# mLSTM's convolution on GpSimd by way of DRAM, its gate scans in HGRN2's sixth chunk, and forget-gate attention's keys placed beside the projections

## The chip, the core and the metric

One NeuronCore of a Trainium2 chip runs the whole program. It has TensorE (matrix products; PE in the rows), VectorE (DVE), ScalarE (ACT), GpSimd (POOL) and SyncE (SP), which here only issues DMA transfers. Each engine runs its own instructions in order and waits on semaphores for the others. TensorE's clock has two levels, 1.2 and 2.4 GHz; the rows give the granted clock of a stretch as a share of the upper one. The metric is the time of one execution in microseconds (us).

## What is computed

The reference is one block with a mixer and a feed-forward part, on 1024 tokens of width 1024. The change touches the mixer alone. A projection of the normalised input gives the inputs of four mixers, each 256 wide (S5, HGRN2, forget-gate attention, mLSTM):

```
def causal_depthwise_conv(x, w):
    k_w, ch = w.shape
    return lax.conv_general_dilated(
        x, w[:, None, :].astype(x.dtype), window_strides=(1,), padding=[(k_w - 1, 0)],
        dimension_numbers=('NWC', 'WIO', 'NWC'), feature_group_count=ch)
...
def mlstm_mixer(q, k, v, o, ig, fz, conv_w, gain):
    bsz, seq, _ = q.shape
    qk = jax.nn.silu(causal_depthwise_conv(jnp.concatenate([q, k], axis=-1), conv_w))
    q_c, k_c = qk[..., :GROUP_W], qk[..., GROUP_W:]
...
    lf = jax.nn.log_sigmoid(fz.astype(F32))
...
    _, h = lax.scan(_mlstm_chunk, init,
                    (heads(q_c), heads(k_c * ML_DH ** -0.5), heads(v), gates(ig), gates(lf)))
```

The convolution has four taps over time, channel by channel, on the 512 channels of mLSTM's queries and keys, and SiLU behind it. The mLSTM gates need running sums and running maxima over the 1024 tokens. HGRN2 is a gated linear recurrence in chunks with 4 heads of 64, forget-gate attention is softmax attention with 4 heads whose scores get the difference of a cumulative log gate, `s = q k / 8 + F[t] - F[s]`.

## The kernel before

Fp32 matrices are split into a high and a low part, and a product is three matmuls (`mm3`, L100 to L102). The input x comes in eight tiles of 128 tokens (`xt`); they are normalised, transposed on TensorE and kept split in SBUF (`aT`), and then all column blocks of the input projection are made from them, in halves of 512 tokens (`gemm_half`: 24 matmuls of 128x512). A generator `g` (`gemms`) yields after each half, so that the caller lays these halves between the steps of the mixers. The order in each engine's queue is that of the program, partly rearranged by a scheduler that respects priorities. A projected block is copied out of PSUM by ScalarE, is transposed if its mixer wants the other layout (`keep_tm`, L403, copies the transposed block), and goes to DRAM scratch (`d_mqk` for mLSTM's queries and keys, `d_fk` and `d_fq` for the attention's, `d_gate` for the gates).

The stage of HGRN2 is the loop over eight chunks of 128 tokens: `hg_scores` (key transposes L832, 56 score products L840), a half of the projection, `hg_out` of the chunk before, another half, `hg_products` (L858 to L868). The level decays (`hlev`) are differences of the scanned log gate (`hb`, L776) made by GpSimd (L790, L791; 28 subtractions for a quarter of 256 tokens), an exponential by ScalarE, and products by VectorE (L797, L799). Quarters are prepared two chunks ahead.

Into this loop mLSTM's preparation is laid: `ml_gates` (rows of 1024 tokens on 4 partitions, VectorE scans L948 and L950) in chunk 0, `ml_conv` for one of the four feature tiles of 128x1024 in each of the chunks 1 to 4, and `ml_columns` (gate rows to columns, L985 and L992) in chunk 5. `ml_conv` loads the tile (`mraw`), scales it by the last tap (L928) and adds the three other taps (L930) on VectorE, takes tanh on ScalarE (L931), makes the SiLU product on VectorE (L932) and scales it on GpSimd (L934). The result stays in SBUF in `mqk0` and `mqk1`. After the loop mLSTM's chunks 0 to 2 run between the last halves of the projection (`ml_scores`: L1018 transposes a tile of keys), then the projections' memory is released and forget-gate attention's pool takes it (`fox_prep`: raw keys `f_kr`, their split `fkA`, the gate row on all partitions `fFB`, values `fv`; L1086 to L1089). `fox_tile` loads eight times four heads' queries (`f_qr`, L1102), splits them (`f_Q`, L1104 and L1105) and makes scores (`at_s`, L1110).

At the start, the constants are loaded on SyncE's queue, then two blocks of weights and x; the tiles of x lie where the constants' raw rows lay. The reciprocal root is made by VectorE in eleven small steps (L61 to L67, `rsq_a`, `rsq_y`), the scaling of x is L117, the transposition L129.

## Time and profile before

| | |
|---|---|
| median of 3 runs | 2910.1 us (2907.98 to 2913.05) |
| the profiled execution | 2912.16 us, span 2910.40 us |
| TensorE (PE) busy | 2664.5 us, 92% of the span |
| weight load (PEld) busy | 2249.0 us, 77% |
| VectorE (DVE) busy | 1836.6 us, 63% |
| ScalarE (ACT) busy | 1221.5 us, 42% |
| GpSimd (POOL) busy | 714.1 us, 25% |

The span is the time from the first to the last instruction that the profiler recorded; the shares are means over stages of different kinds, so that a stage has to be looked at by itself. A busy TensorE need not be at the full clock.

### The profile page before, as it was taken

Reading aid. Unit: us, or ns where it says so; the run is one execution under the profiler, and the core shown is the slowest. Engines: PE = TensorE matmul, PEld = TensorE weight load, DVE = VectorE, ACT = ScalarE, POOL = GpSimd, SP = SyncE. Lnnn points to the kernel's source line nnn. Section 1 sums busy time; section 2 is a strip of 40 time slices with the busy share of each in tenths; the row PEclk is TensorE's granted clock in tenths of the full one; section 3 lists DMA queues with packets and bytes.
Section 4 is the critical chain, followed back from the end, with each engine's and each line's share of the span. In section 5 each row is a group of like instructions: output and inputs, shape, how many; then the busy total and the mean of one; then the engine's idle time right before and its main releaser. Section 6 shows DMA issues by size and latency. Waiting matters only on the chain. (4 is left out here: it accounts for less than half of the span.)

```text
span 2910.4 us, 44979 instructions
## 1 busy us (share of the span) xinstructions
PE 2664.5 (92%) x16607; PEld 2249.0 (77%) x16607; DVE 1836.6 (63%) x4443; ACT 1221.5 (42%) x2362; POOL 714.1 (25%) x839
## 2 busy tenths in 40 slices
PE   6999679899999999899999999999999999699884
PEld 5677558787899878899878787888887888587773
DVE  7523885666888866989563362665653265876665
ACT  4315432344444564444643251444333122465553
POOL 6221520000577511787001000000000100322211
PEclk9899789789999999999999999999999999899997
DMA  4334332423332334323444543511113464799995
GB/s 134 76 95 120 87 92 65 131 70 132 124 112 92 109 124 130 117 88 105 138 120 119 132 122 89 130 57 48 51 35 119 175 209 151 232 305 299 314 301 194
DMA packets 336050, 388.65 MB, mean 134 GB/s; under 512 B 46962, under 2 KB 276220, under 8 KB 335684
## 3 DMA queue, kind: packets, MB, share of 16 engines
q1 hardware_dynamic: 322404, 355.65, 39.5%
q0 software_dynamic: 13280, 29.58, 3.6%
q8 instruction: 132, 2.16, 0.3%
q14 instruction: 90, 0.74, 0.1%
q10 hardware_dynamic: 144, 0.52, 0.0%
HBM read 326.83 MB, written 79.77 MB: 140 GB/s over the span
## 5 line engine op out<-in xcount | busy, mean ns | idle before, releaser
L78 DVE TENSOR_TENSOR f_w<-f_wr,f_w 128x512 fp32r<-128x512 f32 x264 | 292.6, 1135 | 55.3 <-ACT f_w L76 53.9
L100 PE MATMUL g_ps<-a_hi,wh 128*128 128x512 f32 (+1 forms) x648 | 265.8, 410 | 4.9 <-ACT wh L76 4.3
L102 PE MATMUL g_ps<-a_hi,wl 128*128 128x512 f32 (+1 forms) x648 | 260.5, 402 | 1.8 <-DVE wl L78 1.8
L101 PE MATMUL g_ps<-a_lo,wh 128*128 128x512 f32 (+1 forms) x648 | 260.1, 401 | 0.0
L76 ACT ACTIVATE f_w<-f_wr 128x512 fp32r<-128x512 f32 x264 | 158.7, 624 | 175.7 <-POOL f_wr L1324 55.6
L100 PE MATMUL f_ps<-t,f_w 128*128 128x256 f32 x704 | 203.4, 289 | 15.6 <-DVE c L1308 11.9
L102 PE MATMUL f_ps<-t,f_w 128*128 128x256 f32 x704 | 202.5, 288 | 6.5 <-DVE f_w L78 6.5
L101 PE MATMUL f_ps<-t,f_w 128*128 128x256 f32 x704 | 200.8, 285 | 0.0
L1558 ACT ACTIVATE at_sb<-at_sb,at_m 128x256 f32<-128x256 f32 (+7 forms) x224 | 142.2, 635 | 132.5 <-DVE at_m L1556 58.4
L1789 POOL TENSOR_TENSOR o<-o,on 128x256 f32<-128x256 f32 x32 | 24.5, 765 | 623.0 <-DVE at_z L1578 294.6
L78 DVE TENSOR_TENSOR wl<-wr,wh 128x1024 fp32r<-128x1024 f32 (+1 forms) x61 | 74.0, 1215 | 128.7 <-ACT wh L76 128.5
L100 PE MATMUL e_gps<-e_wh,e_xTh 128*128 128x256 f32 x528 | 153.7, 291 | 0.0
L100 PE MATMUL f_ps<-b,f_w 128*128 128x256 f32 x528 | 150.1, 284 | 3.1 <-ACT f_w L76 1.5
L101 PE MATMUL e_gps<-e_wl,e_xTh 128*128 128x256 f32 x528 | 150.8, 286 | 1.4 <-DVE e_wl L78 1.4
L100 PEld LDWEIGHTS f_ps<-t,f_w 128*128 128x128 f32 x704 | 136.6, 194 | 20.0 <-issue 15.8
L102 PE MATMUL f_ps<-b,f_w 128*128 128x256 f32 x528 | 149.4, 283 | 2.7 <-DVE f_w L78 2.7
L102 PE MATMUL e_gps<-e_wh,e_xTl 128*128 128x256 f32 x528 | 150.5, 285 | 0.0
L101 PE MATMUL f_ps<-b,f_w 128*128 128x256 f32 x528 | 149.3, 283 | 0.0
L100 PEld LDWEIGHTS g_ps<-a_hi,wh 128*128 128x128 f32 (+1 forms) x648 | 124.1, 191 | 31.8 <-ACT wh L76 5.0
L102 PEld LDWEIGHTS g_ps<-a_hi,wl 128*128 128x128 f32 (+1 forms) x648 | 123.7, 191 | 28.3 <-DVE wl L78 2.6
L102 PEld LDWEIGHTS f_ps<-t,f_w 128*128 128x128 f32 x704 | 136.6, 194 | 9.9 <-DVE f_w L78 9.8
L101 PEld LDWEIGHTS g_ps<-a_lo,wh 128*128 128x128 f32 (+1 forms) x648 | 124.1, 191 | 23.7
(688 smaller groups left out, 7763.2 us busy)
## 6 DMA issues: line engine op xcount, KB each, us to landing
e_wg<-in_w_gate_e_dram SPq DMA_DIRECT2D x33, 1024.0 KB
e_wu<-in_w_up_e_dram SPq DMA_DIRECT2D x33, 1024.0 KB
e_wd<-in_w_down_e_dram SPq DMA_DIRECT2D x33, 1024.0 KB
wr<-in_w_in_dram SPq DMA_DIRECT2D x60, 512.0 KB
f_dr<-in_w_ffn_down_dram SPq DMA_DIRECT2D x52, 512.0 KB
f_wr<-in_w_ffn_gate_dram SPq DMA_DIRECT2D x44, 512.0 KB
f_wr<-in_w_ffn_up_dram SPq DMA_DIRECT2D x44, 512.0 KB
Q<-qd SPq DMA_DIRECT2D x64, 256.0 KB
```

The lines of the kernel that those rows point to most:

```text
L76: a = self.nc.scalar.activation(hi, raw, AF.Copy)
L78: return a, (eng or self.nc.vector).tensor_tensor(lo, raw, hi.bitcast(F32), ALU.subtract)
L100: nc.tensor.matmul(ps, lh, rh, start=(j == 0), stop=False)
L101: nc.tensor.matmul(ps, lh, rl, start=False, stop=False)
L102: self.last_mm = nc.tensor.matmul(ps, ll, rh, start=False, stop=(j == n - 1))
L1558: nc.scalar.activation(p, p, AF.Exp, bias=m[:, hd:hd + 1], accum_out=z[:, hd:hd + 1])
L1789: nc.gpsimd.tensor_tensor(o4, o4, on, A)
```

## The change

The convolution is made by GpSimd alone but for the tanh, a tile in each of the chunks 0 to 3: a scaling for each tap into a second tile, an addition for the three shifted ones, one operation that makes 0.5 or 0.0625 times (tanh + 1), and one product. The result goes to new DRAM scratch `d_mqc`; `ml_rows` loads it back into `mqk0` and `mqk1` after the loop, in a pool that takes over HGRN2's memory. `ml_gates` is called in chunk 5 and not in chunk 0, `ml_columns` after the loop. `fox_prep` is called before the projections' memory is released, in a pool of its own (`foxk`) on the other side, with two buffers for the raw keys. Two smaller edits: the first four x tiles are loaded on ScalarE's queue, into memory that no longer overlaps the constants' (the two pools change places), and `keep_tm`'s 24 copies out of PSUM are made by ScalarE.

```diff
-                            tmp, early = pool("n_tmp", stack=t_), pool("n_w", 2, stack=t_)
+                            early, tmp = pool("n_w", 2, stack=t_), pool("n_tmp", stack=t_)
...
-                                nc.sync.dma_start(xt, x[t * P:(t + 1) * P, :])
+                                (nc.scalar if t < 4 else nc.sync).dma_start(xt, x[t * P:(t + 1) * P, :])
...
+                            with self.seq():
+                                self.hg_scores(d, c)
+                            decays()
+                            if c < 4:
+                                self.ml_conv(mlt, c)
+                            elif c == 5:
+                                self.ml_gates(mlt)
...
-                        if c == 0:
-                            self.ml_gates(ml, mlt)
-                        elif c < 5:
-                            self.ml_conv(ml, mlt, c - 1)
...
-                        if c == 5:
-                            with self.seq():
-                                self.ml_columns(ml)
+                            self.hg_out(d, NT - 1)
+                    hg_.close()
+                    mp = pool("ml")
+                    self.ml_rows(mp)
                     with self.seq():
-                        self.hg_out(d, NT - 1)
-                mp = pool("ml2")
+                        self.ml_columns(mp)
+                fk = pool("foxk")
...
+                self.fox_prep(fk)
 
             self.pe_last = None
             self.att = pool("fox", 3, side="right")
-            self.fox_prep()
...
-            nc.vector.tensor_copy(o, ps)
+            nc.scalar.copy(o, ps)
...
+        for j in range(4):
+            nc.sync.dma_start(self.mqk[j // 2][:, j % 2], self.d_mqc[j])
...
-        V = nc.vector
-        V.tensor_scalar(dst, src, w(3), None, op0=M)
+        G.tensor_scalar(dst, src, w(3), None, op0=M)
         for d in range(1, 4):
-            V.scalar_tensor_tensor(dst[:, d:], src[:, :T - d], w(3 - d), dst[:, d:], op0=M, op1=A)
+            G.tensor_scalar(t, src, w(3 - d), None, op0=M)
+            G.tensor_tensor(dst[:, d:], dst[:, d:], t[:, :T - d], A)
         nc.scalar.activation(src, dst, AF.Tanh, scale=0.5)
-        V.scalar_tensor_tensor(dst, src, 1.0, dst, op0=A, op1=M)
-
-        G.tensor_scalar(dst, dst, 0.5 * (0.125 if j >= 2 else 1.0), None, op0=M)
...
+        G.tensor_scalar(src, src, 1.0, 0.5 * (0.125 if j >= 2 else 1.0), op0=A, op1=M)
+        G.tensor_tensor(dst, dst, src, M)
+        nc.sync.dma_start(self.d_mqc[j], dst)
```

In the changed file the lines of mLSTM stand six lower (L931 is L936) and HGRN2's one lower (L812 is L813). The first place is ScalarE's queue at the start of HGRN2's chunk 2, where the tanh of a convolved tile (`mraw`) stands. Before, tanh of the first tile:

```order
L902 ACTIVATE hn_sq<-ho 128x256
L762 ACT_TABLE_LOAD
L762 ACTIVATE ht_3390<-ht_3390 128x512
L360 COPY g_raw<-g_ps 128x512
L931 ACT_TABLE_LOAD
L931 ACTIVATE mraw<-mqk_2343 128x1024
L875 COPY hoS<-o_ps 128x256
L768 ACTIVATE hz<-hz 128x512
```

After, tanh of the second tile, behind the exponential of the quarter's levels (`hlev`):

```order
L876 COPY hoS<-o_ps 128x256
L794 ACTIVATE hlev<-hlev 128x1792
L805 ACTIVATE hqe<-hb 128x256
L936 ACTIVATE mraw<-mcv 128x1024
L809 ACTIVATE hebl<-hb 128x2
L813 ACTIVATE hke<-hke 128x256
L361 COPY g_raw<-g_ps 128x512
L404 COPY gs<-g_tp 128x512
L834 COPY hkT<-kT_ps 128x256
```

The tanh's input is now made by GpSimd (`mcv`), and the key decay (`hke`), the copies of projected blocks (`g_raw`, `gs`) and the transposed keys (`hkT`) stand behind it.

The second place is TensorE's queue at the end of the loop, from HGRN2's last output transpose (`oT_ps`) on. Before:

```order
L868 MATMUL o_ps<-hP,hvc 64x64 x2
L888 MATMUL oT_ps<-ident,hoS 128x128 x2
L1018 MATMUL mk_ps<-ident,mqk_2343 128x128 x2
L1023 MATMUL me_ps<-mMx,msel 128x128
L1024 LDWEIGHTS identb
```

After:

```order
L889 MATMUL oT_ps<-ident,hoS 128x128 x2
L990 MATMUL mc_ps<-ident,mrows 128x128 x8
L998 MATMUL md_ps<-mdec,msel_4245 128x8
L998 MATMUL md_ps<-mdec,msel_4248 128x8
L1024 MATMUL mk_ps<-ident,mqk_4222 128x128
L1029 MATMUL me_ps<-mMx,msel 128x128
```

The columns (`mc_ps`, `md_ps`) now stand between HGRN2's last output and mLSTM's first use of `mqk`, and no half of the projection does; `mqk` is a new tile that the four loads fill.

The third place is VectorE's queue in the changed kernel at HGRN2's chunks 0 and 1, where the mLSTM gate rows (`mrows`, `mmx`, `mR`; the scans are the rows L954 and L956) stand between the masked scores of chunk 0 (`hP`), its state update (`hS`) and the next quarter's gates (`ht`, `hz`):

```order
L844 TENSOR_TENSOR hP<-sc_ps,hmask 128x448
L914 SCALAR_TENSOR_TENSOR mrows<-mrows 4x1024
L953 MEMSET mrows 4x1024
L954 SCALAR_TENSOR_TENSOR mrows<-mrows 4x1024
L765 TENSOR_SCALAR ht_2389<-hz 128x512
L955 TENSOR_TENSOR mrows<-mrows 4x1024
L874 SCALAR_TENSOR_TENSOR hS_1049<-hS_1049,hebl,o_ps 64x64 x2
L874 SCALAR_TENSOR_TENSOR hS_1050<-hS_1050,hebl,o_ps 64x64 x2
L956 SCALAR_TENSOR_TENSOR mmx<-mrows 4x1024
L959 COPY mR<-mmx 4x8
L966 TENSOR_TENSOR mrows<-mrows,mmx 4x1024
```

They stood in the same two chunks before; what the call in chunk 5 did not move is mLSTM's part of these rows.

## Rows read from the trace of the kernel before

**Rows 1.** Busy us of each engine by stretch, clock, DMA share, GB/s

```profile
320.00:330.00 10.00, 1.29 (x12) 0.90 (x12) 9.81 (x34) 4.62 (x8) 3.09 (x2) 0.69 0.50 141
...
370.00:380.00 10.00, 0.41 (x6) 0.43 (x8) 9.81 (x32) 5.57 (x9) 3.23 (x2) 0.58 0.39 114
```

**Rows 2.** TensorE's waits from 40 to 620 us: total, times, longest

```profile
PE sc_ps L840 <- DVE hlev L799: 12.3, 2, 11.7
PE md_ps L992 <- DVE mcols L985: 9.7, 1, 9.7
PE sc_ps L840 <- DVE rsq_a L66: 9.2, 1, 9.2
...
PE at_s L1110 <- ACT f_Q L1104: 3.3, 1, 3.3
```

**Rows 3.** Lines of the convolution on VectorE: min/median/max ns, first and last start

```profile
L928 DVE TENSOR_SCALAR mqk<-mraw,vcol x4: 739/740/916, 315.9 to 383.0; 128x1024 f32<-128x1024 f32 x4
...
L930 DVE SCALAR_TENSOR_TENSOR mqk<-mraw,vcol,mqk x12: 1265/1272/1277, 316.9 to 389.7; 128x1023 f32<-128x1023 f32 x4, 128x1022 f32<-128x1022 f32 x4, 128x1021 f32<-128x1021 f32 x4
...
L932 DVE SCALAR_TENSOR_TENSOR mqk<-mraw,mqk x4: 1216/1222/1227, 324.4 to 395.3; 128x1024 f32<-128x1024 f32 x4
```

**Rows 4.** The copy of the transposed block, the same columns

```profile
L403 DVE COPY gs<-g_tp x24: 658/682/692, 99.9 to 516.2; 128x512 f32<-128x512 f32 x24
```

**Rows 5.** GpSimd's operations of 128x1024: by line, and by group (busy us, mean ns)

```profile
L934 POOL TENSOR_SCALAR mqk<-mqk x4: 2760/2766/2791, 325.8 to 396.6; 128x1024 f32<-128x1024 f32 x4
...
L78 POOL TENSOR_TENSOR e_wl<-e_wg,e_wh 128x1024 fp32r<-128x1024 f32 x2 | 4.7, 2354 | 0.0
L600 POOL COPY s5u<-s5u 128x1024 f32<-128x1024 f32 x2 | 2.3, 1188 | 13.7 <-DMA s5u<-tm_u 13.7
```

**Rows 6.** GpSimd's level subtractions, group of 258 to 470 us

```profile
L790 POOL TENSOR_TENSOR hlev<-hb 128x128 f32<-128x128 f32 x42 | 24.2, 576 | 5.9 <-DVE hb L776 5.8
```

**Rows 7.** Timeline of TensorE at chunks 2 and 4: start us, us, instruction

```profile
317.65 0.27 PE L832 MATMUL kT_ps<-ident,hke 128*128 128x128 f32 x1
...
339.12 0.51 PE L858 MATMUL o_ps<-heads,hpd 128*128 128x2 f32 x4
...
366.62 0.27 PE L832 MATMUL kT_ps<-ident,hke 128*128 128x128 f32 x1
```

**Rows 8.** Timeline of VectorE beside GpSimd's scaling from 325.8 us

```profile
326.10 0.72 DVE L66 SCALAR_TENSOR_TENSOR rsq_a<-rsq_a,ms 128x4 f32<-128x4 f32 x1
...
327.89 0.15 DVE L66 SCALAR_TENSOR_TENSOR rsq_a<-rsq_a,ms 128x4 f32<-128x4 f32 x1
```

**Rows 9.** Line of HGRN2's scans: min/median/max ns

```profile
L776 DVE TENSOR_TENSOR_SCAN hb<-ones,ht x16: 391/433/5510, 105.7 to 402.3; 128x128 f32<-128x128 f32 x16
```

**Rows 10.** Timeline of TensorE at mLSTM's first scores

```profile
461.71 0.38 PE L1018 MATMUL mk_ps<-ident,mqk 128*128 128x128 f32 x2
```

**Rows 11.** Stretches of 520 to 550 us, columns as in rows 1

```profile
520.00:530.00 10.00, 9.40 (x68) 8.11 (x68) 6.70 (x27) 2.60 (x6) 0.11 (x1) 0.76 1.01 312
530.00:540.00 10.00, 5.02 (x30) 3.95 (x28) 7.76 (x34) 5.00 (x9) 0.65 (x2) 0.67 0.89 248
540.00:550.00 10.00, 6.84 (x35) 6.07 (x36) 6.51 (x24) 3.55 (x11) 0.66 (x3) 0.50 0.38 107
```

**Rows 12.** DMA issues of 258 to 470 us: count, size, us to landing

```profile
ymix<-s5g POOLq DMA_DIRECT2D x1, 1024.0 KB, 5.7
```

**Rows 13.** Timeline of SyncE's queue at the first queries

```profile
528.89 9.57 SPq L1102 DMA_DIRECT2D f_qr<-fm_fq  x8
```

**Rows 14.** Timeline of the start

```profile
6.36 1.97 SPq L245 DMA_DIRECT2D xt<-in_x_dram  x4
...
16.89 1.06 ACT L113 ACTIVATE n_sq<-xt 128x1024 bf16<-128x1024 f32 x1
...
19.26 1.22 DVE L78 TENSOR_TENSOR wl<-wr,wh 128x1024 fp32r<-128x1024 f32 x1
...
23.71 1.14 PE L129 MATMUL n_ps<-ident,xt 128*128 128x128 f32 x3 [17.38 <-DVE xt L117]
```

More of the change, by code (lines that the diff above doesn't have):

```diff
@@ L229, in block1a @@
             self.sm = pool("sm")
-            with ExitStack() as gem:
+            with ExitStack() as gem, ExitStack() as hg_:
                 right = lambda name, bufs=1, stack=gem: pool(name, bufs, stack=stack, side="right")
@@ L294, in block1a @@
                         next(g)
-                ml = pool("ml")
-                with ExitStack() as b_:
-                    hgb = right("hg2", stack=b_)
-                    mlt = pool("mlt", stack=b_)
-                    self.ml_rows(ml)
-                    for c in range(NT):
-                        if c % 2 == 0:
-                            q = c // 2 + 1
-                            steps = self.hg_quarter(q, hga if q % 2 == 0 else hgb, quarters[q]) if q < 4 else iter(())
-                        d = quarters[c // 2]
-                        with self.seq():
-                            self.hg_scores(d, c)
-                        decays()
-                        if c == 0:
-                            self.ml_gates(ml, mlt)
-                        elif c < 5:
-                            self.ml_conv(ml, mlt, c - 1)
-                        if c:
-                            with self.seq():
-                                self.hg_out(quarters[(c - 1) // 2], c - 1)
-                        next(g)
-                        with self.seq():
-                            self.hg_products(d, c)
-                        decays()
-                        if c < 7:
-                            next(g)
-                        if c == 5:
-                            with self.seq():
-                                self.ml_columns(ml)
@@ new lines, in block1a @@
+                with ExitStack() as m_:
+                    mlt = right("mlt", stack=m_)
+                    with ExitStack() as b_:
+                        hgb = right("hg2", stack=b_)
+                        for c in range(NT):
+                            if c % 2 == 0:
+                                q = c // 2 + 1
+                                steps = self.hg_quarter(q, hga if q % 2 == 0 else hgb, quarters[q]) if q < 4 else iter(())
+                            d = quarters[c // 2]
+                            with self.seq():
[5 more added lines that the diff above has]
+                                self.ml_gates(mlt)
+                            if c:
+                                with self.seq():
+                                    self.hg_out(quarters[(c - 1) // 2], c - 1)
+                            next(g)
+                            with self.seq():
+                                self.hg_products(d, c)
+                            decays()
+                            if c < 7:
+                                next(g)
+                        with self.seq():
+                            self.hg_out(d, NT - 1)
+                    hg_.close()
+                    mp = pool("ml")
+                    self.ml_rows(mp)
@@ L942, in ml_gates @@
         li, lf, F, t1 = (rows[32 * j:32 * j + 4] for j in range(4))
-        Mx = self.mMx[0:4]
+        Mx = self.mmx = mx.tile([4, T], F32, name="mmx")
         nc.sync.dma_start(li, self.d_gate[4:8])
@@ L950, in ml_gates @@
         V.tensor_tensor_scan(Mx, li, li, 0.0, ALU.max, ALU.max)
-        R = sm.tile([4, 9], F32, name="mR")
+        R = mx.tile([4, 9], F32, name="mR")
         V.memset(R[:, 0:1], 0.0)
@@ L962, in ml_gates @@
         V.tensor_scalar(Mx, Mx, -1.0, None, op0=M)
-        dec = self.mdec = sm.tile([4, 8], F32, name="mdec")
+        dec = self.mdec = mx.tile([4, 8], F32, name="mdec")
         V.tensor_tensor(dec, R[:, 0:8], R[:, 1:9], S)
@@ L1083, in fox_prep @@
         for hd in range(4):
-            raw = at.tile([P, T], F32, tag="at_sb", name="f_kr")
+            raw = at.tile([P, T], F32, tag="raw", name="f_kr", bufs=2)
             for d in range(2):
```

18 lines of the change are left out of this document (10 added, 8 removed).

## The prediction

> **What bounds the kernel now.** I read the table of engines first (TensorE is busy for 92% of the span), then the table of 10 us stretches, and only then the waits of TensorE up to 620 us, the part that the change can reach. In the HGRN2 stage (263 to 461 us) TensorE does not bound: in the stretches of [rows 1] it is nearly idle while VectorE is busy for all of the ten microseconds, and the granted clock has fallen to 0.69 and 0.58. The waits say for what TensorE stands [rows 2]: 12.3 us for level decays (`hlev`), 9.7 for mLSTM's columns (`mcols`), 9.2 behind a small reciprocal root (`rsq_a`), all VectorE's. A stage in which VectorE is full is one that gains from work taken off VectorE, unless what takes it over is later than VectorE was. The second place is the start of forget-gate attention, where TensorE waits for queries (`f_Q`, 3.3 us in the same group) and the clock is low.
>
> All sums are against the profiled execution (2912.2 us, span 2910.4); it lies 2.1 us above the median of the three runs, so a difference is taken from 2910.1. Faster and slower mean by more than 0.2% (5.8 us), about what a measurement of this kernel can tell from no change.
>
> **1. The convolution.** On VectorE a tile costs one scaling, three multiply-adds and one product [rows 3]: 0.74 + 3 x 1.27 + 1.22 = 5.8 us, four times 23 us. Eight of the 24 transposed copies of 0.68 us [rows 4] fall into this stage and go to ScalarE: 5.4 us more. VectorE loses about 28 us.
>
> On GpSimd a tile is five scalings and four additions or products of 128x1024. The nearest rows [rows 5]: its scaling takes 2.77 us, the two-input product 2.35, a plain copy of the size 1.19. I take the first two, since they are the very operations: 5 x 2.77 + 4 x 2.35 = 23.3 us a tile, 93 us for four. The lower end is the copy's price with the product's, 5 x 1.19 + 4 x 2.35 = 15.4 us. The Trainium skill (GPSIMD Engine Reference, section 3.1) puts a one-input pass at 1.8 cycles an element at best and a two-input one at 2.6; an estimate from that page at its 1.2 GHz is 1.54 and 2.22 us, or 16.6 us a tile. The scaling's row of 2.77 us disagrees, and the row decides.
>
> What it moves onto the path is the tanh. It stands in ScalarE's queue in program order, and behind it, in the rows of the order shown above, stand the key decay and the copies that TensorE needs next. It can run when GpSimd has done seven of the nine operations, 4 x 2.77 + 3 x 2.35 = 18.1 us. GpSimd's chain: the first tile's input is there at about 259 (an estimate: the load is queued behind a store that was issued at 256), tanh(0) at 278 and the tile's end at 284, with the 1.1 us of the S5 store in it; the quarter's difference and 28 level subtractions at 0.36 pitch (10 us; [rows 6] have 0.58 where VectorE's gate scans ran beside them) to 301; conv(1) to tanh(1) at about 320, tanh(2) 23.3 + 5 later at 349, then levels, and tanh(3) at 386.
>
> Against TensorE's own times before [rows 7]: it began chunk 2's scores at 317.7 and was then held by `hlev` to about 332. Now it comes there some 10 us earlier, waits for tanh(1) and goes on at about 323: 9 us ahead. Tanh(2) stands ahead of the weight split for chunk 3, which had its products at 339 in chunk 2 and would be in chunk 3's projection at 343: it waits to 355, so chunk 3 ends 5 us behind. Tanh(3) stands ahead of chunk 4's key decay: TensorE began those scores at 366.6, was held to 382 by `rsq_a`, and is now held to 388: 8 us behind. From there VectorE is free of convolution, the 9.7 us wait for `mcols` is gone because the columns are made after the loop, and the last quarter's levels come 4 us earlier than they did: -8 + 9.7 + 3 = about +4.5 us at chunk 7's scores. New waits of some 42 us stand in for 40 us of old ones.
>
> What the two engines do to each other comes off that. While the GpSimd scaling that starts at 325.8 runs, a four-column VectorE operation took 0.72 us, and 0.15 later beside the same scaling [rows 8]; a scan, 0.43 us at the median, took 5.5 beside a run of short GpSimd subtractions [rows 9]. Of 36 long operations I let one in five or so cost the path its 0.57 us: 4 to 5 us. The term is therefore **0**, with ends of -20 (all 36 times 0.57 on the path) and +26 (four tiles at 15.4 instead of 23.3, 4 x 7.9 = 31 us, of which 26 is TensorE's).
>
> The Trainium skill (SBUF — State Buffer, Who interferes with whom) says that a VectorE instruction with two SBUF inputs and a GpSimd instruction that reads SBUF exclude each other, and that the first holds the ports for its whole length. By that rule all 93 us of the convolution would be closed to such VectorE work. The trace agrees in part: the scan was held to the end of the run, the small operation for 1.07 of 2.79 us only.
>
> **2. The way through DRAM.** The convolved tiles are written while the loop runs; each write waits on SyncE's queue for its tile, ahead of projections' stores and of loads that are wanted a chunk later (20 us), and that chunk is the cover. Without it, a load that lands behind GpSimd's tile would cost up to the 5 us of the last two operations, which stands in A's width. They are loaded back into memory that HGRN2's tiles held, so the loads can't start before chunk 7's products (about 460). Before, mLSTM's first scores began at 461.7 without a wait [rows 10], with the tiles in place; now all four parts are needed in the first chunk, and in TensorE's queue nothing but the columns stands in between. Four times 512 KB at the 312 GB/s which the busiest stretch moved [rows 11] are 6.7 us, and 2 us of issue and first landing: **-8 us**. Bounds: the 1 MB store of S5's result took 5.7 us [rows 12], so 11.4 for 2 MB; below, -4, if the two parts that `mk` needs come first and TensorE does something with them.
>
> **3. Gate scans.** The order says they stay: the rows of VectorE's order above still have all three mLSTM scans' work ahead of chunk 1's products. Only the forget-gate attention's cumulative gate goes to the sixth chunk, because its buffer follows the fourth tile. What moves (about 5 us of VectorE) is in the sum of part 1; the 4 to 5 us of columns after the loop lie beside the reload. **0.**
>
> **4. Keys beside the projections.** Before, the keys' loads, their splits and the queries' loads come all at once after the last projection, since their pool takes the memory of the projections' input. The queries' eight issues begin at 528.9 and take 9.6 us, behind all others, in a stretch where the DMA engines are full [rows 11, 13]. TensorE is idle for 0.6 + 5.0 + 3.2 = 8.7 us of 520 to 550, at clocks of 0.76, 0.67 and 0.50 [rows 11]. Its work there is 9.4 x 0.76 + 5.0 x 0.67 + 6.8 x 0.50 = 13.9 us at the full clock, so the most there is to gain is 16 us. With keys in place only the queries have to come after the last transposition; the first scores stand some 35 instructions earlier in TensorE's order. The softmax's own chain remains, and the clock has to come back: **+11 us**, bounds +4 (the wait for `f_Q` and a little more, without the clock) and +16.
>
> **5. The start.** TensorE starts at 23.7, and ends a chain: loads of x issued at 6.4, last square sum 16.9, reciprocal root, with two weight splits of 1.2 us between its steps (the first at 19.3), scaling [rows 14]. Now the x tiles are the first on ScalarE's queue, their memory is free from the start, and the splits stand behind the scaling. The splits alone are 2.4 us; the load is issued some 5 us sooner, of which I count 2, because constants are needed too and land later. **+4.5 us**, bounds +2 and +6.
>
> **Sum:** 0 - 8 + 0 + 11 + 4.5 = 7.5 us faster; 2910.1 - 7.5 = 2902.6, say **2903 us**.
>
> **The rivals.** *A: as above*, with the terms' smaller errors 2890 to 2912.
> *B: GpSimd is as quick as its copy.* Tanh comes 5 to 8 us earlier each time, part 1 gives +26: 2877, I say 2880. For it: the copy of 1.19 us. Against: four scalings within 1% of 2.77 us.
> *C: the shared path of VectorE and GpSimd decides, and it gets slower.* Place: the two quarters' level bursts, where 28 pairs of VectorE products meet conv(1) to conv(3). If each of 36 long operations holds VectorE for the 0.57 us of the row and all are on the path, part 1 is -20 and the whole 12 to 13 us slower: 2923. It decides from about 15 of the 36 on (7.5 / 0.57 = 13 undo the gain). For it: VectorE is busy for 0.98 of the stretches of [rows 1], and the 5.5 us scan. Against: VectorE has 28 us less to do, and once past the first 1.07 us it ran beside the scaling undisturbed. The skill's rule stands behind this case.
> *D: it does not do what it says.* The scans stay (part 3), and the keys' gain is eaten by the queries, which still wait for the projections' memory: without part 4's clock gain (+4), the sum is +0.5, 2909.6.
>
> **How the numbers follow.** A 0.45, B 0.17, C 0.28, D 0.10. Faster: B whole, two thirds of A: 0.47. Same: the rest of A and most of D: 0.22. Slower: C and a little of A and D: 0.31. The range that leaves two in ten out goes from B to C, 2878 to 2926; A's own is 2890 to 2912.
>
> **What would show it.** TensorE's first transposition at 18.5 to 20 us. GpSimd scalings of 2.77 and products of 2.35, a tile 23 to 24 us (C: 28 and more; B: under 18). Waits of TensorE in chunks 2, 3 and 4 of 12 to 16 us for the key decay and the weight split, with tanh as what ScalarE stands at, and no 9.7 us wait for `mcols`. A wait of 7 to 9 us for the reload at 460. First attention scores 12 to 18 us earlier, with 520 to 550 at a clock above 0.8. I am wrong if the HGRN2 stage alone moves by more than 10 us either way, or if the reload has lost its wait.

## The result and the profile after

| | before | after |
|---|---|---|
| median (range, runs) | 2909.0 us (2907.1 to 2913.1, 4) | 2940.6 us (2939.9 to 2944.4, 4) |
| profiled span | 2910.4 us | 2942.6 us |

The changed kernel is slower: ratio 1.0109, 95% interval 1.0092 to 1.0127. That is 15 us beyond the upper end of the range, and on the side that the forecast took for less likely.

The first line of the page of the changed kernel, busy time of each engine: VectorE has 16 us less than before and GpSimd 75 us more. By the rows of before, some 39 us of work left VectorE (23 of convolution and 24 copies of 0.68), so that the rest of its work takes longer than it did.

```profile
PE 2668.1 (91%) x16590; PEld 2250.8 (76%) x16607; DVE 1820.7 (62%) x4400; ACT 1231.8 (42%) x2386; POOL 789.5 (27%) x871
```

Where the time went is read from TensorE's timeline at places that both kernels have. Each row gives the first start, and how far the changed kernel is behind by then.

| first start of | before | after | behind |
|---|---|---|---|
| TensorE's first transposition (L129) | 23.7 | 22.2 | -1.5 |
| S5's first product (`bl_ps`) | 139.9 | 144.5 | +4.6 |
| HGRN2's stage (first `kT_ps`) | 263.9 | 275.2 | +11.3 |
| its last output transpose (`oT_ps`) | 461.4 | 491.7 | +30.3 |
| mLSTM's first use of `mqk` (`mk_ps`) | 461.7 | 498.3 | +36.6 |
| the attention's first scores (`at_s`) | 539.4 | 563.3 | +23.9 |
| the next normalisation (`n_ps`) | 653.7 | 681.0 | +27.3 |
| end of the span | 2910.4 | 2942.6 | +32.2 |

So the path lost 11.3 us up to the start of HGRN2's stage, 19.0 in it (the stage is 216.5 us long and was 197.5) and 6.3 at the reload, won 12.7 between the reload and the attention, and lost 8.3 of that again behind it.

The stretches of the changed kernel, columns as in [rows 1]. From 330 to 340 us ScalarE does nothing at all, VectorE and TensorE less than half, and GpSimd alone is full. From 520 to 550 us TensorE is full at the whole clock, where [rows 11] had 0.76, 0.67 and 0.50.

```profile
320.00:330.00 10.00, 2.14 (x29) 1.75 (x29) 9.75 (x21) 1.97 (x2) 9.82 (x4) 0.50 0.00 0
330.00:340.00 10.00, 4.15 (x31) 2.67 (x31) 4.61 (x23) 0.00 (x0) 9.73 (x4) 0.50 0.10 28
...
520.00:530.00 10.00, 10.00 (x63) 8.11 (x60) 5.64 (x12) 4.66 (x9) 0.10 (x1) 1.00 0.46 132
...
540.00:550.00 10.00, 10.00 (x64) 8.31 (x63) 5.45 (x24) 1.92 (x4) 0.25 (x2) 1.00 0.15 40
```

TensorE's waits from 40 to 620 us in the changed kernel answer [rows 2]. The key decay (`hke`), which had no row there, takes 36.9 us; the wait for `mcols` is gone. The two waits for a weight split (`wh`) both lie before HGRN2.

```profile
PE kT_ps L833 <- DVE hke L814: 36.9, 5, 19.0
PE g_ps L100 <- ACT wh L76: 11.2, 2, 6.0
PE sc_ps L841 <- DVE hlev L800: 8.9, 7, 6.3
PE sc_ps L841 <- DVE rsq_a L65: 7.0, 1, 7.0
```

VectorE's group of the key decay has 3.8 us of idle time before it, behind ScalarE's exponential; for the rest of the 36.9 its queue has to be followed back. The timeline of the changed kernel, by start, with the idle time before a row and its releaser in brackets:

```profile
341.51 1.06 ACT L936 ACTIVATE mraw<-mcv 128x1024 f32<-128x1024 f32 x1 [14.15 <-POOL mcv L935]
342.48 0.40 ACT L805 ACTIVATE hqe<-hb 128x256 f32<-128x256 f32 x1
...
342.91 1.07 DVE L806 TENSOR_TENSOR hqe<-hqe,hq 128x256 f32<-128x256 f32 x1 [8.30 <-ACT hqe L805]
343.90 3.07 DVE L814 TENSOR_TENSOR hke<-hke,hz 128x256 f32<-128x256 f32 x1
347.02 0.48 PE L833 MATMUL kT_ps<-ident,hke 128*128 128x128 f32 x1 [10.83 <-DVE hke L814]
...
371.10 1.06 ACT L936 ACTIVATE mraw<-mcv 128x1024 f32<-128x1024 f32 x1 [6.83 <-POOL mcv L935]
...
373.48 0.51 ACT L771 ACTIVATE ht<-ht,lb 128x256 f32<-128x256 f32 x1
374.02 2.27 DVE L773 TENSOR_TENSOR ht<-ht,ht 128x512 f32<-128x512 f32 x1 [7.12 <-ACT ht L771]
376.74 2.33 DVE L777 TENSOR_TENSOR_SCAN hb<-ones,ht 128x128 f32<-128x128 f32 x4
378.37 0.43 POOL L791 TENSOR_TENSOR hlev<-hb 128x128 f32<-128x128 f32 x1 [0.68 <-DVE hb L777]
...
397.63 0.37 ACT L876 COPY hoS<-o_ps 128x256 f32<-128x256 f32 x1 [9.38 <-DVE hS L874]
397.94 1.70 ACT L794 ACTIVATE hlev<-hlev 128x1792 f32<-128x1792 f32 x1
...
410.03 1.06 ACT L936 ACTIVATE mraw<-mcv 128x1024 f32<-128x1024 f32 x1 [10.09 <-POOL mcv L935]
...
411.09 0.40 ACT L813 ACTIVATE hke<-hke 128x256 f32<-128x256 f32 x1
411.52 0.98 DVE L814 TENSOR_TENSOR hke<-hke,hz 128x256 f32<-128x256 f32 x1 [3.83 <-ACT hke L813]
412.55 0.47 PE L833 MATMUL kT_ps<-ident,hke 128*128 128x128 f32 x1 [18.96 <-DVE hke L814]
...
431.55 0.91 ACT L771 ACTIVATE ht<-ht,lb 128x256 f32<-128x256 f32 x2
433.33 1.27 POOL L780 TENSOR_TENSOR hpd<-hq,hz 128x512 f32<-128x512 f32 x1 [9.49 <-DVE ht L773]
...
455.06 0.37 ACT L876 COPY hoS<-o_ps 128x256 f32<-128x256 f32 x1 [8.80 <-DVE hS L874]
455.33 1.70 ACT L794 ACTIVATE hlev<-hlev 128x1792 f32<-128x1792 f32 x1
457.70 1.19 PE L841 MATMUL sc_ps<-hlev 64*64 64x64 f32 x10 [6.32 <-DVE hlev L800]
```

It reads as a circle through three engines (tiles and tanh are counted from 0). ScalarE stands 14.2 us at tanh(1) until GpSimd has summed the tile; the exponentials of chunk 2 stand behind it, VectorE is idle for 8.3 us and TensorE waits 10.8. Tanh(2) then holds the second half of the third quarter's gates (`ht`), so that VectorE scans them at 376.7. The levels on GpSimd start behind that scan, at 378.4, although GpSimd itself had been busy with tile 2 until 375.7, and tile 3 stands behind the levels. So tanh(3) comes at 410.0, and behind it the key decay for which TensorE waits 19.0 us. Of these, tanh(3) alone holds little: VectorE was idle for only 3.8 us before its product. Until 407.7 it made the second half of the levels, whose exponential (397.9) had stood behind an output row (`hoS`) that waited 9.4 us for VectorE. The last turn is the longest: behind tanh(3) ScalarE comes to the last quarter's gates at 431.6, GpSimd is idle for 9.5 us until they are made, the levels' second exponential stands behind an output row again, and TensorE waits 6.3 us for the levels.

GpSimd's operations of 128x1024 in the changed kernel, a line of the code each (ns min/median/max, first and last start). A tile takes 23.6 to 26.9 us from its first operation to its last, where 23 to 24 was forecast. One scaling (L938), which does two operations with two numbers in the instruction, takes about a third of those that read a number for each partition from SBUF (L934). The numbers' place alone is not the reason: the scaling of before has its one number in the instruction and takes 2.77 [rows 5].

```profile
L934 POOL TENSOR_SCALAR mct<-mraw,vcol x12: 2833/2850/3712, 274.6 to 404.8; 128x1024 f32<-128x1024 f32 x12
...
L938 POOL TENSOR_SCALAR mraw<-mraw x4: 1039/1043/1255, 293.8 to 411.2; 128x1024 f32<-128x1024 f32 x4
L939 POOL TENSOR_TENSOR mcv<-mcv,mraw x4: 2341/2358/2403, 295.1 to 412.3; 128x1024 f32<-128x1024 f32 x4
```

### The profile page after: what moved, and what is told of

It reads as the page before. It is cut to its first block, busy times and chain, and to the rows that moved or that the text cites. A ratio compares the mean times of both kernels' runs of the same rounds, so it can differ in the third digit from the quotient of the medians.

```text
span 2942.6 us, 44998 instructions
## 1 busy us (share of the span) xinstructions
PE 2668.1 (91%) x16590; PEld 2250.8 (76%) x16607; DVE 1820.7 (62%) x4400; ACT 1231.8 (42%) x2386; POOL 789.5 (27%) x871
## 5 line engine op out<-in xcount | busy, mean ns | idle before, releaser
L100 PE MATMUL e_gps<-e_wh,e_xTh 128*128 128x256 f32 x528 | 152.8, 289 | 0.0
L101 PEld LDWEIGHTS g_ps<-a_lo,wh 128*128 128x128 f32 (+1 forms) x648 | 125.8, 194 | 23.7
## 6 DMA issues: line engine op xcount, KB each, us to landing
e_wu<-in_w_up_e_dram SPq DMA_DIRECT2D x33, 1024.0 KB, 14.2
```

Of the source, the lines that this page charges most:

```text
L100: nc.tensor.matmul(ps, lh, rh, start=(j == 0), stop=False)
L101: nc.tensor.matmul(ps, lh, rl, start=False, stop=False)
```

## The experiments

Gains and losses between runs are differences of their ratios to the kernel before, which ran on the same chip, times 2909 us. The changed kernel is 1.0109 (1.0092 to 1.0127). "Stage" is the time from HGRN2's first `kT_ps` to its last `oT_ps`: before 197.5, after 216.5 us.

**Parts put back, one at a time.** The start:

```diff
-early, tmp = pool("n_w", 2, stack=t_), pool("n_tmp", stack=t_)
+tmp, early = pool("n_tmp", stack=t_), pool("n_w", 2, stack=t_)
-(nc.scalar if t < 4 else nc.sync).dma_start(xt, ...)
+nc.sync.dma_start(xt, ...)
```

> The changed kernel with the start put back: x on SyncE's queue, the two early pools in their old places. Theory (order at the start): the changed kernel begins its first transposition 1.5 us earlier but computes S5's constants later, so that GpSimd's powers of S5 run beside VectorE's and HGRN2's weights come late; at S5's blocks it is 4.6 us behind. With the start put back the kernel is about 5 us faster than the changed one, 2935. Rival (the start is a gain, the loss before S5 is the copies on ScalarE): 1.5 us slower, 2942.

1.0087 (1.0066 to 1.0109): 6 us faster, within overlapping intervals, with HGRN2 4.3 us earlier. The traces say it more clearly: in the 13 traces with the changed start S5's first product comes at 141.5 to 144.8 us, in the 6 with the old one at 139.3 to 140.4. The start costs.

```diff
-            nc.scalar.copy(o, ps)
+            nc.vector.tensor_copy(o, ps)
```

> The changed kernel with the 24 copies of transposed blocks put back on VectorE. Theory: on ScalarE they stand behind S5's own copies, which wait for TensorE, and a weight load stands behind their stores on SyncE's queue; this costs 5 us at 230 us. About 5 us faster than the changed kernel, 2935. Rival (the copies relieve VectorE in the HGRN2 stage and that is worth as much): no change within 2 us, 2940.

1.0069 (1.0051 to 1.0088): 12 us faster, 6.0 of them before HGRN2; its stage is as long (216.3), although VectorE has 5 us of copies back in it.

The convolution's arithmetic back on VectorE, with everything else of the change:

```diff
-        G.tensor_scalar(dst, src, w(3), None, op0=M)
+        V.tensor_scalar(dst, src, w(3), None, op0=M)
         for d in range(1, 4):
-            G.tensor_scalar(t, src, w(3 - d), None, op0=M)
-            G.tensor_tensor(dst[:, d:], dst[:, d:], t[:, :T - d], A)
+            V.scalar_tensor_tensor(dst[:, d:], src[:, :T - d], w(3 - d), dst[:, d:], op0=M, op1=A)
...
```

> The changed kernel with the convolution's arithmetic back on VectorE, in the changed places (chunks 0 to 3), still by way of DRAM. Theory (the HGRN2 stage lost 19 us to the convolution on GpSimd): 15 to 20 us faster than the changed kernel, 2921 to 2926. Rival (VectorE is the bound of the stage, so that GpSimd's share of the work was a gain and the loss is elsewhere): no faster than 2938.

0.9987 (0.9973 to 1.0001): 35 us faster and level with the kernel before, although HGRN2 still begins 8.7 us late; its stage of 182.4 makes up for that. The three gains add up to more than the 32 us that the change lost, so they are not independent. The largest hangs on the convolution's engine. What about it?

**Tanh, time or shared path.** Tanh left out:

```diff
-        nc.scalar.activation(src, dst, AF.Tanh, scale=0.5)
```

> The changed kernel without the four tanh of the convolution; GpSimd's nine operations per tile stay, in the same order. Leaves the SiLU's tanh out. Theory (ScalarE's queue stands behind the tanh, which waits 39.6 us in all for GpSimd): the waits of TensorE for the key decay (36.9 us) go, the stage gains 12 to 18 us, 2923 to 2929. Rival (the path that VectorE and GpSimd share): the waits stay or move to VectorE, the gain is under 5 us, 2936 or more.

1.0132 (1.0102 to 1.0162), stage 219.8: no gain at all. The theory that ScalarE's queue alone does it fell. VectorE's and GpSimd's timeline of that run shows what took its place:

```profile
360.21 2.17 DVE L777 TENSOR_TENSOR_SCAN hb<-ones,ht 128x128 f32<-128x128 f32 x4
...
372.75 2.34 POOL L938 TENSOR_TENSOR mcv<-mcv,mraw 128x1024 f32<-128x1024 f32 x1
375.05 1.26 POOL L780 TENSOR_TENSOR hpd<-hq,hz 128x512 f32<-128x512 f32 x1
376.27 0.40 POOL L791 TENSOR_TENSOR hlev<-hb 128x128 f32<-128x128 f32 x1
```

The third quarter's scan is there 16.5 us sooner than in the changed kernel, and its levels start 2 us sooner: two tiles, 1 and 2, stand ahead of them on GpSimd. Freed from one queue, the same work waits in the other.

The long operations as fills of the same length (convolution left out):

```diff
-            G.tensor_scalar(t, src, w(3 - d), None, op0=M)
-            G.tensor_tensor(dst[:, d:], dst[:, d:], t[:, :T - d], A)
+            G.memset(t, 0.5)               # 128x3072
+            G.memset(t[:, 0:2560], 0.5)
...
```

> The changed kernel with GpSimd's long operations of the convolution, but for the first and the SiLU's scaling, replaced by fills of a wide tile that take about as long (2560 to 3072 elements, some 2.4 to 2.9 us) and read nothing from SBUF. Leaves the convolution's taps and the last product out. Theory (GpSimd's time and the queues that wait for it: levels, tanh, stores): the HGRN2 stage stays long, over 200 us from the first key transpose to the last output (changed kernel 216, before 197), time 2930 or more. Rival (the SBUF path that VectorE and GpSimd share): the fills don't read, so VectorE is free; stage under 192 us, 2915 or less.

1.0027 (1.0013 to 1.0041), stage 192.3: 24 us faster. This spoke for the shared path of VectorE and GpSimd, and I took it so until the order of the rows was compared: with fills only one tile stands ahead of the third quarter's levels, and ScalarE waits 2.1 us at tanh, not 39.6. Nor do fills leave VectorE free: it is busy for 144.0 us of this stage, and for 142.8 with the convolution's 23 us on it.

The convolution called in chunks 1, 2, 4 and 6:

> The changed kernel with the convolution's tiles called in chunks 1, 2, 4 and 6. The order on GpSimd is the same for the first two tiles, the third tile's end and the middle of the fourth stand behind the quarters' levels, and the second tanh stands behind the key decay instead of ahead of it. Theory (waits of the queues behind GpSimd): TensorE waits less for the key decay (36.9 us in the changed kernel) and the third and fourth quarter's levels come earlier: 10 to 20 us faster than the changed kernel, 2920 to 2930. Rival (the shared path): the same operations run beside the same work, no change, 2938 to 2943.

1.0095 (1.0078 to 1.0112), stage 216.7. It decided nothing: the scheduler put tiles 1 and 2 ahead of the third quarter's levels again (scanned by 359.7 us, levels from 373.5).

Six of the seven fills of a tile made to read SBUF again:

```diff
-            G.memset(t, 0.5)
-            G.memset(t[:, 0:2560], 0.5)
+            G.tensor_scalar(t[:, 0:T], t[:, T:2 * T], 0.5, None, op0=M)
+            G.tensor_tensor(t[:, 0:T], t[:, T:2 * T], t[:, 2 * T:], A)
...
```

> As in the run with fills, the convolution on GpSimd is replaced by operations of about the same length, but here five of the eight long ones of a tile read SBUF again (a scaling of 2.8 us or a sum of 2.3 us over 128x1024) and only the others fill; the convolution itself is left out. If VectorE is slowed by what GpSimd reads and writes (the shared path), the HGRN2 stage is 205 us or longer and the whole 2930 or more, and a key decay product on VectorE (line 814 of the changed kernel) takes 0.8 us or more in the mean. If it was the time of GpSimd alone, that is levels that wait behind the convolution, the stage is 192 us and the whole 2914, as with fills.

1.0120 (1.0095 to 1.0145), stage 215.7. The time is the one forecast for the shared path, but the run does not separate the two. ScalarE's wait at tanh and VectorE's line of the key decay in that run:

```profile
ACT mraw L941 <- POOL mcv L940: 35.1, 4, 12.0
...
L814 DVE TENSOR_TENSOR hke<-hke,hz 128x256 f32<-128x256 f32 x6 | 2.7, 455 | 0.0
```

The product takes 0.46 us, as with fills (0.44), and not the 0.8 that the shared path wanted; but tanh stands ahead of the exponentials again, and two tiles stand ahead of the third quarter's levels.

Work that nobody uses behind each tile of the kernel with the convolution on VectorE (the levels made to follow it), filling or reading:

```diff
+        for _ in range(4):      # d_fill: memsets of 128x3072 and 128x2560
+            G.tensor_scalar(t[:, 0:T], t[:, T:2 * T], 0.5, None, op0=M)
+            G.tensor_tensor(t[:, 0:T], t[:, T:2 * T], t[:, 2 * T:], A)
```

> The changed kernel with the convolution's arithmetic back on VectorE (2903 us, stage of 182 us), and behind each tile eight fills of 2.7 and 2.3 us on GpSimd, 20 us a tile, whose result nobody uses; the next quarter's levels are made to stand behind them. Shared path: fills read nothing, so VectorE is not slowed and the only price is levels that come later; stage under 195 us, whole under 2912. GpSimd's time alone: the levels come 20 us later in three quarters, the stage is 200 us or more and the whole 2920.

> The same, but the eight operations behind each tile are scalings and sums of 128x1024 in SBUF of 2.8 and 2.35 us, whose result nobody uses. Shared path: at least 10 us slower than with fills, most of it in the HGRN2 stage, where the same VectorE lines take longer each. GpSimd's time alone: within 3 us of the run with fills.

1.0131 (1.0106 to 1.0156) with fills, 1.0142 (1.0115 to 1.0170) with reads; stages 219.4 and 225.6. Twenty useless microseconds a tile ahead of the levels cost 42 us over the 0.9987 without them; reading adds 3 us, which the intervals don't tell from nothing. The 42 us are not shown to be GpSimd's time alone. The two stages without and with the fills, columns as in [rows 1], have 361 VectorE instructions each:

```profile
272.60:455.00 182.40, 148.80 (x1447) 121.95 (x1445) 142.84 (x361) 86.26 (x133) 60.13 (x99) 0.89 0.37 110
272.10:491.50 219.40, 150.30 (x1447) 122.53 (x1445) 175.31 (x361) 92.00 (x137) 149.94 (x138) 0.82 0.32 92
```

Beside the fills VectorE takes 32 us longer for them (182.9 us with reads), so that fills are no control for what GpSimd does to VectorE.

**The order.** GpSimd's queue alone: tiles 1 to 3 behind the levels of their quarter.

```diff
-if c < 4:
-    self.ml_conv(mlt, c)
+if c == 0:
+    self.ml_conv(mlt, 0)
+elif c % 2 and c < 6:
+    with tc.issue_after(self.lev_last.ins):   # last level subtraction
+        self.ml_conv(mlt, (c + 1) // 2)
```

> The changed kernel with one thing different: GpSimd's order. Tiles 1, 2 and 3 of the convolution are called in chunks 1, 3 and 5 and kept behind the levels of quarters 1, 2 and 3, so that one tile and not two stands between two bursts of levels. Every operation is kept. If the loss comes from GpSimd's and ScalarE's queues (levels behind two tiles, key decay and scan inputs behind a tanh that waits for its tile), the HGRN2 stage goes from 216 us to 195 or less and the whole to 2920 or less. If it comes from the shared path of VectorE and GpSimd, the same 36 long operations still run beside VectorE, and the whole stays at 2932 or more.

1.0149 (1.0133 to 1.0165), stage 220.4: no gain, the time that was expected for the shared path. The rows show a queue all the same. ScalarE's timeline there:

```profile
396.02 1.06 ACT L939 ACTIVATE mraw<-mcv 128x1024 f32<-128x1024 f32 x1 [21.03 <-POOL mcv L938]
...
397.54 1.70 ACT L797 ACTIVATE hlev<-hlev 128x1792 f32<-128x1792 f32 x1
...
399.54 0.40 ACT L816 ACTIVATE hke<-hke 128x256 f32<-128x256 f32 x1
```

The levels are made in time, and then their exponential stands behind a tanh that waits 21 us for a tile that is now later: 63.8 us at four tanh, where it was 39.6. Its counterpart with fills:

> The run with the new order of GpSimd, and the long operations replaced by fills of the same length that read nothing (the convolution is left out, its tanh stays). Order and lengths are alike, so that what is left is the shared path: by the shared path as the main cause at least 15 us less than with the real convolution; by the queues as the main cause at most 6 us less.

1.0039 (1.0021 to 1.0057), stage 186.0, with 4.8 us at tanh. ScalarE's order came out differently again, so that the 32 us between the two are not the shared path's alone.

Both queues: the same order, and tanh with the two last operations kept behind the quarter's last key decay on ScalarE.

```diff
+if c % 2 and c < 6:
+    with tc.issue_after(self.ke_last.ins):    # last exponential of the key decay
+        self.ml_conv_tail(*cv)                # tanh, scaling, product, store
...
```

> The new order of GpSimd as before (one tile behind the levels of each quarter), and with it tanh and the two last operations of tiles 1 to 3 kept behind the last key decay of the quarter on ScalarE's queue, so that no tanh stands ahead of an exponential that TensorE needs. All operations are kept. Two queues as the cause (levels on GpSimd, exponentials on ScalarE, each enough by itself to hold the stage): ScalarE's wait at tanh no longer holds the key decay, the stage is 198 us or less and the whole 2922 or less. The shared path as the main cause: GpSimd's operations still run beside VectorE, stage 208 or more, whole 2932 or more.

> The same order of GpSimd and ScalarE with fills in place of the long operations (the convolution is left out). What it gains over the run with the real convolution in the same order is the price of the shared path: by the queues as the cause at most 8 us, by the shared path 15 us or more.

1.0051 (1.0032 to 1.0071), stage 198.5: 17 us less than the changed kernel, with every operation kept. The last quarter's levels end 147 us into the stage, where it is 173 in the changed kernel and 151 before. The fills in this order give 1.0025 (1.0012 to 1.0037), stage 192.1: reading and the rest of the difference are 8 us, and the intervals overlap a little. In TensorE's waits and ScalarE's timeline with both queues freed, the key decay (L820 here) has fallen from 36.9 to 20.6 us, and tanh(2) stands behind both exponentials:

```profile
PE kT_ps L839 <- DVE hke L820: 20.6, 4, 13.4
...
382.56 1.70 ACT L800 ACTIVATE hlev<-hlev 128x1792 f32<-128x1792 f32 x1
...
384.56 0.40 ACT L819 ACTIVATE hke<-hke 128x256 f32<-128x256 f32 x1
390.56 1.06 ACT L947 ACTIVATE mraw<-mcv 128x1024 f32<-128x1024 f32 x1 [5.60 <-POOL mcv L941]
```

**What is worth keeping.** Start, copies and convolution put back (the three edits above together), so that of the change only the way through DRAM, the gates' place and the keys stay; and the same with the keys back in the projections' memory:

> The changed kernel with start, copies and the convolution's engine put back; the way through DRAM, the gates' place and the keys beside the projections stay. Theory (the losses add up, the keys' gain stays): 2885 to 2895, faster than before by 12 to 22 us. Rival (start and copies were costly only together with the convolution on GpSimd): 2898 to 2904, as with the convolution alone put back.

> As best_dram, but forget-gate attention's keys are prepared after the projections again, in their memory. Theory (the keys beside the projections gain about 13 us, as the traces suggest: 36.6 us behind at the first mLSTM scores, 24 at the first attention scores): 10 to 14 us slower than best_dram. Rival (the keys' loads were hidden anyway or the queries' wait takes their place): within 5 us.

0.9976 (0.9963 to 0.9990), 2899.7 us: faster than both kernels, stage 189.5, and 3 us below the run with the convolution alone put back, as its rival had it: the start and the copies, which gained 6 and 12 us beside the convolution on GpSimd, gain little without it. HGRN2 begins 8 us earlier than in that run, and its stage is 7 us longer. With the keys back in the projections' memory 0.9986 (0.9973 to 0.9999), 2903.2 us. TensorE's first attention scores in the two:

```profile
525.28 0.31 PE L1116 MATMUL at_s<-fkA,f_Q 128*128 128x128 f32 x1
```

```profile
547.59 0.48 PE L1115 MATMUL at_s<-fkA,f_Q 128*128 128x128 f32 x1 [9.53 <-ACT f_Q L1109]
```

They are 22 us apart here, 16 at the next normalisation (643.5 and 659.5) and 3.5 in the medians, with intervals that overlap: the rival's "within 5 us".

The convolution on GpSimd with the better order, start and copies put back:

> The new order of GpSimd, with the start and the transposed copies put back as they were before the change: the convolution stays on GpSimd, keys stay early, the reload stays. By the queues: about 20 us less than the run with the new order alone, 2895 to 2903, level with or below the 2900 of the kernel that has the convolution on VectorE. By the shared path: 2912 or more.

> The run with both queues in the new order, and the start and the transposed copies as they were before the change. By the two queues 2895 to 2905, by the shared path 2912 or more.

1.0098 (1.0084 to 1.0113) and 1.0058 (1.0038 to 1.0079); stages 222.3 and 205.2. The second was to reach 2895 to 2905, and its median is 2928.4, with runs from 2914.7 to 2939.2. Its HGRN2 stage begins 6.6 us earlier than with the start and copies left as changed, and ends at the same 472.4: TensorE waits 14.3 us for `hlev` of the last quarter, whose second exponential stands on ScalarE behind an output row (`hth`) that waits 8.9 us for VectorE. That this row takes the gain was not tried. Both runs came out on the side that was expected for the shared path (2912 or more), and neither tells it from such a queue.

## Why the prediction was wrong

By its own signs the prediction was wrong twice: the HGRN2 stage moved by 19 us and not by less than 10, and the reload lost its wait.

**Part 1, the convolution: forecast 0, measured -19.** This is the step that failed, and it failed in three terms: GpSimd's chain is 10 us later than was let, the last quarter's levels, counted as a gain of 3 us, lose some 10, and VectorE is relieved by 5 us where 28 were counted (case C). GpSimd's operations were right (2.85 and 2.36 us, 23.6 to 26.9 a tile) but for the one scaling of 1.04. TensorE against the kernel before, each counted from its own stage's start, at key transposes (`kT_ps`):

| place | forecast | measured |
|---|---|---|
| chunk 2 goes on (second transpose) | 9 ahead | 2.7 behind |
| end of chunk 3 (first transpose of chunk 4) | 5 behind | 10.4 behind |
| chunk 4 goes on (second transpose) | 8 behind | 17.6 behind |
| chunk 6, the wait for `mcols` gone | 2 ahead | 9.1 behind |
| chunk 7 | 4.5 ahead | 18.9 behind |

Tanh(1) came 66 us into the stage and not 56. Two of these 10 us are the first tile's end, 5 the second quarter's levels and 3 the second tile. GpSimd stands idle for 8.8 us ahead of the levels, until the quarter's gates and their scan are there; [rows 6] already had 5.9 us `<-DVE hb`. VectorE comes to them behind mLSTM's gate rows, among them a scan (L956) of 4.36 us that takes 2.3 in the run with the convolution on VectorE, so that here too the shared path may have a part. The forecast gave 17 us from the tile's end to the levels' end; its named terms fill 11 of them, so that some of that wait may be in it, and 22 were needed. The delay then stays: tanh(2) came at 96 and not 85, tanh(3) at 135 and not 122.

The second term is the levels of the last quarter. I had them 4 us earlier than before and let TensorE go free from chunk 4 on. They end 173 us into the stage, where they ended at 151, since the gates that they are made of stand behind tanh(3): between chunk 6's first and second transpose TensorE loses 10 us. The forecast had no case in which a late tanh makes the next levels later.

The mechanism, tanh in ScalarE's queue with the key decay behind it, was right for chunk 2 (8.3 of 10.8 us). In chunk 4 it holds VectorE for 3.8 of TensorE's 19.0 us, and the wait for the weight split in chunk 3 is not there.

Shown by runs: freeing ScalarE alone (tanh left out) or GpSimd alone (order) gives nothing, freeing both gives 17 us and a stage of 198.5, 1 us from before. That is the 0 of the forecast, but for an order which the kernel doesn't have. Which link of the circle carries how much of the 17 us is read from the rows and not shown by a run of its own. Nor is it the end of the reckoning, since with the convolution on VectorE the stage is 182.4: of the 16 us between the two, no run says what is GpSimd's time and what the shared path.

**Case C, the shared path.** Its time was the nearest of the four, and its reason is not cleared. The stage of the changed kernel, to be held against the row with 142.84 above:

```profile
275.20:491.70 216.50, 151.77 (x1447) 124.30 (x1446) 148.09 (x340) 91.27 (x137) 134.51 (x130) 0.82 0.32 93
```

The 23 us of convolution left VectorE, and it is busy for 5 us longer: its other 340 instructions take some 25 us more. Against the kernel before (152.8 us in its stage) the relief is 4.7 us and not 28. The forecast's 4 to 5 us were what I let of this reach the path. How much does was not isolated, because fills hold VectorE as long as reads (150.1 and 151.1 us in the two runs with both queues freed). These two still differ by 8 us (1.0051 against 1.0025); that is what reading costs more than writing, as far as the order of their rows is the same, and not the price of all contention.

The Trainium skill (SBUF — State Buffer, Who interferes with whom) says that two-input VectorE work is shut out by GpSimd instructions that read SBUF, not by those that only write. The trace agrees in one row: the key decay's product took 3.07 us at 343.9, beside a GpSimd product. Its mean of six does not follow reading: 0.98 in the changed kernel, 0.46 in the run with reads, and 0.41 with both queues freed, with reads as with fills. Fills hold other VectorE operations (a scaling of 128x4 took 3.25 us beside one at 335.0 us of the first run with fills).

**Part 2, the reload: forecast -8, measured -6.3** to `mk_ps` and -9.0 to the first scores. The size was near. The rows give the wait to another owner:

```profile
491.24 1.74 SPq L920 DMA_DIRECT2D mqk<-fm_mqc  x4
491.70 0.44 PE L889 MATMUL oT_ps<-ident,hoS 128*128 128x128 f32 x2 [1.74 <-ACT hoS L876]
...
497.43 0.99 PE L998 MATMUL md_ps<-mdec,msel 4*128 4x8 f32 x4 [3.63 <-DVE msel L997]
498.34 0.47 PE L1024 MATMUL mk_ps<-ident,mqk 128*128 128x128 f32 x1
```

TensorE waits here for the columns (`msel`), and has no wait left for `mqk`, whose loads took 3.9 us. The columns that part 3 laid beside the reload are as long as the reload itself, so that the size came out for a reason that was not the forecast's. What the one costs without the other was not tried.

**Part 4, the keys: forecast +11, measured +12.7** from `mk_ps` to `at_s`, and the clock of 520 to 550 us is 1.00. The error is behind it: I ended the sum at the first scores. 8 us are lost again by the end, and in the pair with and without early keys 22 us shrink to 3.5. From 650 to 700 us the clock is 0.83 (0.93 before), and the next normalisation waits 6.0 us for `f_x`, where the kernel before waited 4.1; what else gives it back is open.

**Part 5, the start: forecast +4.5, measured -4.6 at S5's first product.** The first transposition is 1.5 us earlier; 18.5 to 20 us was forecast, and it came at 22.2. The first square sum starts at 10.3 and not at the 16.9 of [rows 14] (its last one, there), but the fourth at 17.6: between them ScalarE makes two weight splits (13.5 and 15.5). And I followed that chain alone; beside the early loads of x the constants on SyncE's queue are issued later:

```profile
0.80 4.98 ACTq L245 DMA_DIRECT2D xt<-in_x_dram  x4
7.19 0.32 SPq L168 DMA_DIRECT2D dsk<-in_s_d_dram  x1
22.22 2.68 PE L129 MATMUL n_ps<-ident,xt 128*128 128x128 f32 x8 [12.09 <-DVE xt L117]
28.57 0.21 ACT L463 ACTIVATE s5s<-s5s 128x8 f32<-128x8 f32 x1
```

`dsk` was issued at 4.32 before, and S5's first sine (L463, before L462) ran at 15.61; now it runs at 28.57. What TensorE loses is a wait for weight splits: from 20 to 150 us it waits 6.0 us for `wh` and 2.9 for `wl`, where it was 2.6 and 1.0, and with the start put back it is 2.6 and 1.0 again. What makes the splits late was not followed.

**The 24 copies** were counted as 5.4 us off VectorE and nothing else. ScalarE makes them late, since they stand behind S5's copies, which wait for TensorE; a store that waits for one on SyncE's queue went out at 222.5 and not at 210.4, the weight load behind it at 226.5 and not at 214.5, and TensorE waits 5.2 us for `wh` at 236.7, where it waited 1.7. With the copies put back the two go out at 214.7 and 218.7, and the wait is 1.7 again. That is 6 us before HGRN2; the rest of that run's 12 us comes behind 680 us, and I have no row for it.

**Part 3** held: the scans stayed where they were. The forget gate's rows, which did move, stand on ScalarE from 422.9 to 427.9 us, ahead of the last quarter's gates; what that costs was not tried.

## What to carry to other kernels

When long work moves to an engine that also feeds the bounding engine, draw every queue that the moved work's helper steps stand in, and follow one late step around all of them to its own next instance. An experiment that frees one queue and gains nothing doesn't clear that queue: look at what the freed work waits for next, and free both. And compare the order of the rows, and the busy time of the engine that is to be spared, before you take a run for a control: here fills changed a scheduler's order and held VectorE as long as reads did, so that their 24 us are the price of neither.

## What the runs showed of the hardware

A GpSimd scaling of 128x1024 took 2.85 us where it reads a number for each partition, 2.77 with one number in the instruction ([rows 5]), and 1.04 where it does two operations with two numbers in the instruction; no run shows why. The Trainium skill (GPSIMD Engine Reference, section 3.1) gives 2.6 cycles an element for two inputs; an estimate from it at the page's 1.2 GHz is 2.2 us, and the products' 2.36 are near it. Beside GpSimd's long operations a VectorE product of 0.41 us took up to 3.07 (L814), and over the stage some 25 us went this way; beside the first run's fills it was some 20. The granted clock was 0.50, the lower of the two levels, from 320 to 350 us, where TensorE was busy for 2 to 4 of ten microseconds, and 1.00 from 520 to 550, where it had no gap.
